# Merged activations of a hybrid decoder layer: VectorE block transposes and a trip through DRAM in place of TensorE transposes

## The chip, the cores and the metric

One core of one Trainium2 chip runs the whole kernel. The metric is the device time of one execution in microseconds. The engines are TensorE (PE in the profile; PEld is its weight load), VectorE (DVE), ScalarE (ACT), GpSimd (POOL) and SyncE (SP, which here only issues DMAs). Every engine works through its own list in order; they meet through semaphores.

## The reference, cut to what matters

One layer of three parallel token mixers over 256 tokens and 2048 channels, each projected to 2048 channels, weighted by a sigmoid gate and added; then one output projection, a residual and a norm:

```
merged = (g_sb * (o_sb @ w_branch_sb[layer])
          + g_ssd * (o_ssd @ w_branch_ssd[layer])
          + g_mem * (o_mem @ w_branch_mem[layer]))
x = x + merged @ w_out[layer]
return rms_norm(x, final_norm_w)
```

All matrices are float32. The kernel forms a product as three TensorE products of parts: `hi` is the value rounded to the type fp32r, `lo` the rest, and the sum is hi*hi + hi*lo + lo*hi.

## The kernel before, in words

**A weight product (`gemm`).** It makes 256 tokens x 512 output columns. Weights stream in chunks of two 128-row tiles (`load_chunk`, 512 KB, line 207, issued by SP into the four buffers `raw`). `split` makes `wh` on ScalarE (line 146) and `wl` on VectorE (line 150), three buffers each; then 12 matrix products follow (lines 266 to 268: with `wh`, `wl`, `wh`). A product over 2048 channels has eight chunks, called c0 to c7 below. The left operand must lie with channels on the partitions ("columns", class `Cols`, as hi and lo).

**What sets the order.** The program is written out once, and each engine keeps that order. `defer(fn, n)` puts a piece of work behind the products of the n-th next chunk; `pump()`, at the end of every chunk, runs what is due. The result of a product is fetched `LATE` = 3 chunks after its last chunk.

**The tail around the change.** The third branch goes through four groups g of 512 columns. For each group there is a gate product (from `hT`, 8 chunks) and a branch product (from `oD`, 8 chunks). `branch_evac` then multiplies the branch product by its gate on VectorE (line 857, two instructions for the two halves t of the tokens, tile `sig`) and adds it to `merged[t]` on GpSimd (line 858). `merged` has tokens on the partitions, so the output projection needs it turned. `merged_cols` does that on TensorE: eight 128x128 transposes a group (line 838, tile `mt` in PSUM), and two chunks later `split` writes `mT` (hi on ScalarE, lo on VectorE). The output projection (`w_out`) has four products over `mT`; its first product follows the branch product of group 3 at once and reads the columns of group 3 in its chunks c6 and c7, those of groups 0 to 2 in c0 to c5. The evacuation and the transposes of group g thus lie inside the first chunks of the product after it: the gate product of group g+1, or for group 3 the first product with `w_out`.

Other DMAs that ScalarE issues in this stretch are the gate bias (`sig`, line 843), the final norm's weights (`fw`, line 879) and the residual (`xr`, line 921). The results are stored at the very end (line 917).

Of the kernel before, what the change touches and what calls it, by code (L numbers as in the profile page):

```python
# [10 lines left out]
F32 = mybir.dt.float32  # L11
# [5 lines left out]
P = 128  # L17
D = 2048
T = 256
NKT = D // P  # L20
GW = 512
# [4 lines left out]
LATE = 3  # L26
# [15 lines left out]
def trunk_kernel(  # L42
# [6 lines left out]
    nc = tc.nc  # L49
# [6 lines left out]
    dram = ctx.enter_context(tc.tile_pool(name="dram", bufs=1, space=bass.MemoryType.DRAM))  # L56
# [5 lines left out]
    def nm(s):  # L62
        cnt[0] += 1
        return f"{s}_{cnt[0]}"

    def slot(shape, dt=F32, n="slot"):
        return big.tile(shape, dt, tag="slot", name=nm(n))

    def t4(shape, n="t4"):
        return tmp.tile(shape, F32, tag="t4", name=nm(n), bufs=2)  # L70
# [16 lines left out]
    def bank(shape, n="bank"):  # L87
        return psB.tile(shape, F32, tag="bank", name=nm(n))
# [11 lines left out]
    ident = const.tile([P, P], F32, name="ident")  # L100
# [41 lines left out]
    def split(*parts):  # L142


        for hi, _, src, scale in parts:
            nc.scalar.activation(hi, src, AF.Copy, **({} if scale is None else {"scale": scale}))  # L146
        for hi, lo, src, scale in parts:
            h32 = hi.bitcast(F32)
            if scale is None:
                nc.vector.tensor_tensor(lo, src, h32, ALU.subtract)  # L150
            else:
                nc.vector.scalar_tensor_tensor(lo, src, scale, h32, ALU.mult, ALU.subtract)
# [19 lines left out]
    def defer(fn, chunks=LATE):  # L172

        cnt[0] += 1
        heapq.heappush(late, (now[0] + chunks, cnt[0], fn))
# [9 lines left out]
    def pump():  # L185


        now[0] += 1
        while late and late[0][0] <= now[0]:
            heapq.heappop(late)[2]()  # L190
        advance(lanes[now[0] % 2])

    def finish():
        while lanes[0] or lanes[1]:
            for lane in lanes:
                advance(lane)
# [8 lines left out]
    def load_chunk(w, c0, width, k0, kc):  # L205
        raw = stage.tile([P, kc, width], F32, tag="raw", name=nm("raw"), bufs=RAWB)
        nc.sync.dma_start(
            raw, w[k0 * P:(k0 + kc) * P, c0:c0 + width].rearrange("(k p) n -> p k n", p=P))
        return raw
# [36 lines left out]
            nc.scalar.activation(dst, acc[:, :, 1], AF.Copy)  # L246
            nc.vector.tensor_tensor(dst, acc[:, :, 0], dst, ALU.add)

    def gemm(lhs, nk, w, c0, evac):

        acc2 = psA.tile([P, 2, GW], F32, tag="acc", name=nm("acc"), bufs=2)
        acc = [acc2[:, 0], acc2[:, 1]]
        kc = KC
        for k0 in range(0, nk, kc):
            raw = load_chunk(w, c0, GW, k0, kc)
            wh = stage.tile([P, kc, GW], F32R, tag="wh", name=nm("wh"))
            wl = stage.tile([P, kc, GW], F32R, tag="wl", name=nm("wl"))
            split((wh, wl, raw, None))
            for j in range(kc):
                kt = k0 + j  # L260
                lh, ll = lhs.at(kt)
                first, last = kt == 0, kt == nk - 1
                for t in range(2):
                    a = acc[t]
                    tt = slice(t * P, (t + 1) * P)
                    nc.tensor.matmul(a, lh[:, tt], wh[:, j], start=first, stop=False)  # L266
                    nc.tensor.matmul(a, lh[:, tt], wl[:, j], start=False, stop=False)  # L267
                    nc.tensor.matmul(a, ll[:, tt], wh[:, j], start=False, stop=last)  # L268
            pump()
        defer(lambda: evac(acc))  # L270

    def to_cols(dst, b0):

# [165 lines left out]
    for g in range(4):  # L439
        gemm_cols(memT, NKT, w_mem_kv, 2 * g * P, to_split_cols(kT, 2 * g),  # L440
                  acc=None if g else [bank([P, 2, T], "acc") for _ in range(2)])
# [161 lines left out]
    for g in range(2):  # L603
        gemm(hT, NKT, w_in, C_SBV + g * GW, to_rows(vS, g * GW))
# [226 lines left out]
    merged = [slot([P, D], F32, "merged") for _ in range(2)]  # L831
    mT = []

    def merged_cols(k0):
        ps = bank([P, 2, T], "mt")
        for j in range(2):
            for t in range(2):
                nc.tensor.transpose(ps[:, j, t * P:(t + 1) * P],  # L838
                                    merged[t][:, (k0 + j) * P:(k0 + j + 1) * P], ident)
        defer(lambda: split((*mT[0].at(k0, 2), ps, None)), 2)  # L840

    def gate_evac(c0, sig):
        nc.scalar.dma_start(sig[:, 0], b_gate[c0:c0 + GW].partition_broadcast(P))
        def evac(acc):
            for t in (1, 0):
                nc.vector.tensor_tensor(sig[:, t], acc[t], sig[:, 0], ALU.add)
            defer(lambda: sigmoid(sig), 1)
        return evac

    def branch_evac(br, g, sig):  # L850
        cs = slice(g * GW, (g + 1) * GW)
        def evac(acc):
            for t in range(2):
                if br == 0:
                    nc.vector.tensor_tensor(merged[t][:, cs], acc[t], sig[:, t], ALU.mult)
                else:
                    nc.vector.tensor_tensor(sig[:, t], acc[t], sig[:, t], ALU.mult)  # L857
                    nc.gpsimd.tensor_tensor(merged[t][:, cs], merged[t][:, cs], sig[:, t],  # L858
                                            ALU.add)
            if br == 2:  # L860
                for pr in range(2):
                    defer(lambda pr=pr: merged_cols(4 * g + 2 * pr), 1)
        return evac

    branches = ((4096, oM, 8, w_branch_mem), (0, oS, 8, w_branch_sb), (2048, None, 16, w_branch_ssd))
    for br, (g0, src, nk, wb) in enumerate(branches):
        for g in range(4):
            sig = t4([P, 2, GW], "sig")
            gemm(hT, NKT, w_in, C_GATE + g0 + g * GW, gate_evac(g0 + g * GW, sig))
            if src is None:  # L870
                finish()
                mT.append(Cols(NKT, "mT"))
                src = oD[0]
            gemm(src, nk, wb, g * GW, branch_evac(br, g, sig))


    yo = [slot([P, D], F32, "yo") for _ in range(2)]
# [58 lines left out]
    g = 3  # L936
# [9 lines left out]
    for t in range(2):  # L946
        tt = slice(t * P, (t + 1) * P)
        for cs in (slice(0, GW),) if t == 0 else (slice(0, T), slice(T, GW)):
            acc = psA.tile([P, 2, GW], F32, tag="acc", name=nm("acc"),
                           bufs=2)[:, 0, 0:cs.stop - cs.start]  # L950
# [50 lines left out]
```

## Time and profile before

| | |
|---|---|
| time of the runs | 1227.94 us median of 3 (1227.71 to 1228.21) |
| span of the profiled execution | 1226.6 us, so 1.3 us below the median time |
| TensorE busy, of the span | 99% |
| VectorE, ScalarE, GpSimd busy | 64%, 53%, 4% |
| mean granted TensorE clock | 0.998 |
| from memory | 239.48 MB, 197 GB/s over the span |

The profile gives for the execution itself only its span; what a run takes beyond it (1.3 us) is the start and the end that the trace does not hold. In the page's groups, `out<-in` names the tile that is written and those that are read; "idle before" is what the engine waited just ahead of an instruction, and the arrow says for whom. The times of matrix products overlap (0.39 us each, one begun every 0.23 us), so the distance between starts is their price, not their duration.

### The profile page before, as it was taken

How to read it: one execution, taken by the hardware profiler on the slowest of the kernel's cores; microseconds unless marked ns; L12 is line 12 of the kernel's file. 1: busy time of each engine (PE TensorE's matmuls, PEld its weight loads, DVE VectorE, ACT ScalarE, POOL GpSimd, SP SyncE). 2: the span in 40 equal slices, each digit the busy share in tenths (PEclk: the TensorE clock that was granted, in tenths of full speed). 3: DMA queues.
4: the chain of work that ended last, by engine and by line, in shares of the span. 5: the costliest groups of instructions: out<-in, count | busy, mean ns of one | idle time of the engine just before them, and what ended most of it. 6: DMA issues, size and time to landing. Idle time of an engine off the chain costs nothing.

```text
span 1226.6 us, 16569 instructions
## 1 busy us (share of the span) xinstructions
PE 1215.5 (99%) x6388; PEld 1034.8 (84%) x6388; DVE 784.2 (64%) x990; ACT 649.1 (53%) x875; POOL 51.2 (4%) x50
## 2 busy tenths in 40 slices
PE   9999999999999999999999999999999999999997
PEld 7888888888888888888888888888888888888886
DVE  5686554565654555888888758676777755555554
ACT  6765443554445454545665756475756544444443
POOL 0000000000000000010100000000000010110101
PEclk9999999999999999999999999999999999999999
DMA  9966566655566656565567667686766666567673
GB/s 340 342 197 187 163 194 189 187 168 165 166 180 182 187 172 182 169 182 173 177 185 223 207 200 218 180 231 181 231 184 192 202 195 205 188 197 240 204 240 107
DMA packets 175023, 242.70 MB, mean 198 GB/s; under 512 B 10272, under 2 KB 109792, under 8 KB 174816
## 3 DMA queue, kind: packets, MB, share of 16 engines
q1 hardware_dynamic: 168224, 229.51, 61.2%
q10 hardware_dynamic: 6720, 12.13, 3.0%
q8 instruction: 50, 0.82, 0.3%
q14 instruction: 29, 0.24, 0.1%
HBM read 239.48 MB, written 2.13 MB: 197 GB/s over the span
## 4 chain that ended last, share of the span: by engine, by line
PE 96%; DMA 1%; issue 1%; DVE 1%; ACT 1%; SPq 0%; POOLq 0%; POOL 0%; ACTq 0%
PE acc L229 29%; PE acc L266 15%; PE acc L267 15%; PE acc L268 15%; PE acc L233 14%; PE acc L398 1%; PE acc L399 1%; PE acc L397 1%; PE y L773 1%; DMA raw<-in_w_out_dram 1%; DMA raw<-in_w_mem_kv_dram 1%; PE dtp L459 0%; PE xp L730 0%; PE mt L838 0%; PE spo L649 0%
## 5 line engine op out<-in xcount | busy, mean ns | idle before, releaser
L150 DVE TENSOR_TENSOR wl<-raw,wh 128x1024 fp32r<-128x1024 f32 (+1 forms) x409 | 502.8, 1233 | 310.3 <-ACT wh L146 308.1
L146 ACT ACTIVATE wh<-raw 128x1024 fp32r<-128x1024 f32 (+1 forms) x409 | 431.0, 1055 | 382.5 <-PE acc L268 200.7
L229 PE MATMUL acc<-hT,wh 128*128 128x512 f32 x1408 | 444.0, 397 | 0.0
L233 PEld LDWEIGHTS acc<-hT,wl 128*128 128x128 f32 x1408 | 264.5, 188 | 62.5
L233 PE MATMUL acc<-hT,wl 128*128 128x256 f32 x1408 | 276.8, 278 | 0.0
L229 PEld LDWEIGHTS acc<-hT,wh 128*128 128x128 f32 x1408 | 214.4, 189 | 0.1
L266 PE MATMUL acc<-wh,hT 128*128 128x512 f32 x448 | 175.9, 393 | 0.0
L267 PE MATMUL acc<-wl,hT 128*128 128x512 f32 x448 | 174.7, 390 | 0.0
L268 PE MATMUL acc<-wh,hT 128*128 128x512 f32 x448 | 174.6, 390 | 0.0
L266 PEld LDWEIGHTS acc<-wh,hT 128*128 128x128 f32 x448 | 84.1, 188 | 17.7 <-ACT sq L146 0.5
L268 PEld LDWEIGHTS acc<-wh,hT 128*128 128x128 f32 x448 | 84.1, 188 | 17.8
L267 PEld LDWEIGHTS acc<-wl,hT 128*128 128x128 f32 x448 | 84.1, 188 | 17.4 <-DVE wl L150 0.6
L266 PE MATMUL acc<-wh,oD 128*128 128x512 f32 x128 | 49.8, 389 | 0.0
L267 PE MATMUL acc<-wl,oD 128*128 128x512 f32 x128 | 49.8, 389 | 0.0
L268 PE MATMUL acc<-wh,oD 128*128 128x512 f32 x128 | 49.8, 389 | 0.0
L687 DVE SCALAR_TENSOR_TENSOR cT<-cu,wcols,cT 128x255 f32<-128x255 f32 (+2 forms) x96 | 46.4, 483 | 3.4
L858 POOL TENSOR_TENSOR merged<-merged,sig 128x512 f32<-128x512 f32 x16 | 25.1, 1588 | 521.9 <-DVE sig L857 521.9
L229 PE MATMUL acc<-memT,wh 128*128 128x512 f32 x128 | 40.5, 398 | 0.0
L266 PE MATMUL acc<-wh,mT 128*128 128x512 f32 x96 | 37.4, 390 | 0.0
L268 PE MATMUL acc<-wh,mT 128*128 128x512 f32 x96 | 37.4, 389 | 0.0
L267 PE MATMUL acc<-wl,mT 128*128 128x512 f32 x96 | 37.4, 389 | 0.0
L630 POOL TENSOR_TENSOR lm<-lm,sp 128x384 f32<-128x384 f32 x8 | 13.1, 1639 | 394.7 <-DVE sp L629 385.0
(250 smaller groups left out, 1301.4 us busy)
## 6 DMA issues: line engine op xcount, KB each, us to landing
raw<-in_w_in_dram SPq DMA_DIRECT2D x288, 512.0 KB, 3.8
raw<-in_w_branch_ssd_dram SPq DMA_DIRECT2D x32, 512.0 KB, 4.1
raw<-in_w_out_dram SPq DMA_DIRECT2D x32, 512.0 KB, 5.1
raw<-in_w_mem_kv_dram SPq DMA_DIRECT2D x31, 512.0 KB, 6.6
raw<-in_w_branch_mem_dram SPq DMA_DIRECT2D x16, 512.0 KB, 4.1
raw<-in_w_branch_sb_dram SPq DMA_DIRECT2D x16, 512.0 KB, 4.5
dec<-acT SPq DMA_DIRECT2D x24, 256.0 KB, 6.2
sig<-in_b_gate_dram ACTq DMA_DIRECT2D x12, 256.0 KB, 4.7
```

The lines of the kernel that those rows point to most:

```text
L146: nc.scalar.activation(hi, src, AF.Copy, **({} if scale is None else {"scale": scale}))
L150: nc.vector.tensor_tensor(lo, src, h32, ALU.subtract)
L229: nc.tensor.matmul(halves[b], wh[:, kt - k0, b * P:(b + 1) * P], lhs.both(kt), start=first, stop=False, skip_group_check=True)
L233: nc.tensor.matmul(halves[b][:, 1], wl[:, kt - k0, b * P:(b + 1) * P], lhs.at(kt)[0], start=False, stop=last, skip_group_check=True)
L266: nc.tensor.matmul(a, lh[:, tt], wh[:, j], start=first, stop=False)
L267: nc.tensor.matmul(a, lh[:, tt], wl[:, j], start=False, stop=False)
L268: nc.tensor.matmul(a, ll[:, tt], wh[:, j], start=False, stop=last)
L397: nc.tensor.matmul(a, lh[:, tt], wh[:, g], start=first, stop=False)
L398: nc.tensor.matmul(a, lh[:, tt], wl[:, g], start=False, stop=False)
L630: nc.gpsimd.tensor_tensor(lm, lm, sp, ALU.subtract)
L687: nc.vector.scalar_tensor_tensor(a[:, s:T], u[:, 0:T - s], convw[:, 3 - s, i:i + 1], a[:, s:T], ALU.mult, ALU.add)
L858: nc.gpsimd.tensor_tensor(merged[t][:, cs], merged[t][:, cs], sig[:, t], ALU.add)
```

## The change

The eight transposes on TensorE go. In their place, for every group: two block transposes on VectorE (`turn`), which turn each 32x32 block in place of its 128x128 tile and write them in the order (t, j, k, c); one DMA of 512 KB to a scratch tensor in DRAM (`away`); four DMAs of 128 KB back, one for each band of 32 partitions (`back`), which put the blocks where a full transpose would have them; and the same split into `mT`, as four pieces of 256 columns in place of two of 512. Runs of 128 numbers (512 bytes) are contiguous in the read back. ScalarE issues all five DMAs. For group 3 alone the evacuation is done two chunks after the product, not three.

```
-    def gemm(lhs, nk, w, c0, evac):
+    def gemm(lhs, nk, w, c0, evac, chunks=LATE):
...
-        defer(lambda: evac(acc))
+        defer(lambda: evac(acc), chunks)
...
-    def merged_cols(k0):
-        ps = bank([P, 2, T], "mt")
-        for j in range(2):
-            for t in range(2):
-                nc.tensor.transpose(ps[:, j, t * P:(t + 1) * P],
-                                    merged[t][:, (k0 + j) * P:(k0 + j + 1) * P], ident)
-        defer(lambda: split((*mT[0].at(k0, 2), ps, None)), 2)
+    turned = [dram.tile([2, P, 4, 4, 32], F32, name=f"turned{i}") for i in range(4)]
+
+    def turn(g):
+
+        pair = slot([P, 2, 1024], F32, "turn")
+        blocks = pair[:, 0].rearrange("p (t j k c) -> p t j k c", t=2, j=4, k=4)
+        cols = pair[:, 1].rearrange("p (i k c) -> p i k c", i=8, k=4)
+        for t in range(2):
+            nc.vector.transpose(blocks[:, t].rearrange("p j k c -> p k j c"),
+                                merged[t][:, g * GW:(g + 1) * GW]
+                                .rearrange("p (k j c) -> p k j c", k=4, j=4))
+
+        def away():
+            nc.scalar.dma_start(turned[g].rearrange("t p j k c -> p t (j k c)"),
+                                blocks.rearrange("p t j k c -> p t (j k c)"))
+
+        def back():
+            for j in range(4):
+                nc.scalar.dma_start(
+                    cols[32 * j:32 * j + 32].rearrange("r i k c -> r i (k c)"),
+                    turned[g][:, :, j].rearrange("t (i r) k c -> r (t i) (k c)", r=32))
+            for k in range(4):
+                defer(lambda k=k: split((*[a.rearrange("p (i c) -> p i c", c=32)
+                                           for a in mT[0].at(4 * g + k)],
+                                         cols[:, :, k], None)), 1 + k // 2)
+        defer(away, 1)
+        defer(back, 2)
...
-                for pr in range(2):
-                    defer(lambda pr=pr: merged_cols(4 * g + 2 * pr), 1)
+                defer(lambda: turn(g), 1)
...
-            gemm(src, nk, wb, g * GW, branch_evac(br, g, sig))
+            gemm(src, nk, wb, g * GW, branch_evac(br, g, sig), 2 if br == 2 and g == 3 else LATE)
```

Where it puts things on ScalarE, in the gate product after group 0's branch product (the splits of the chunks c3 to c7 are the rows `wh`, and the last `wh` is c0 of the product after it). Before:

```order
L146 ACTIVATE wh_8741<-raw_8739 128x1024
L146 ACTIVATE wh_8769<-raw_8767 128x1024
L146 ACTIVATE wh_8787<-raw_8785 128x1024
L146 ACTIVATE mT_8526<-mt_8757 128x2x256
L146 ACTIVATE mT_8526<-mt_8762 128x2x256
L146 ACTIVATE wh_8809<-raw_8807 128x1024
L146 ACTIVATE wh_8827<-raw_8825 128x1024
```

And now:

```order
L146 ACTIVATE wh_8745<-raw_8743 128x1024
L146 ACTIVATE wh_8766<-raw_8764 128x1024
L847 DMA turned_5981<-turn_8761 128x2x512
L146 ACTIVATE wh_8785<-raw_8783 128x1024
L852 DMA turn_8761<-turned_5981 32x8x128 x4
L146 ACTIVATE wh_8807<-raw_8805 128x1024
L146 ACTIVATE mT_8530<-turn_8761 128x256 x2
L146 ACTIVATE wh_8829<-raw_8827 128x1024
L146 ACTIVATE mT_8530<-turn_8761 128x256 x2
L146 ACTIVATE wh_8852<-raw_8850 128x1024
```

Here wh_8745 is c3, so `away` stands behind the split of c4, the four reads behind that of c5, and the first pieces of `mT` behind that of c6 and ahead of that of c7.

On VectorE, in the first product with `w_out`, after group 3 (`sig` is the multiplication by the gate, `wl` the splits of the chunks from c1 on). Before:

```order
L150 TENSOR_TENSOR wl_9647<-raw_9644,wh_9646 128x1024
L150 TENSOR_TENSOR wl_9665<-raw_9662,wh_9664 128x1024
L857 TENSOR_TENSOR sig_9304<-acc_9469,sig_9304 128x512 x2
L150 TENSOR_TENSOR wl_9687<-raw_9684,wh_9686 128x1024
L150 TENSOR_TENSOR wl_9715<-raw_9712,wh_9714 128x1024
L150 TENSOR_TENSOR wl_9733<-raw_9730,wh_9732 128x1024
L150 TENSOR_TENSOR mT_8529<-mt_9702,mT_8529 128x2x256
L150 TENSOR_TENSOR mT_8529<-mt_9707,mT_8529 128x2x256
L150 TENSOR_TENSOR wl_9755<-raw_9752,wh_9754 128x1024
```

And now:

```order
L150 TENSOR_TENSOR wl_9657<-raw_9654,wh_9656 128x1024
L877 TENSOR_TENSOR sig_9312<-acc_9479,sig_9312 128x512 x2
L150 TENSOR_TENSOR wl_9679<-raw_9676,wh_9678 128x1024
L842 STREAM_TRANSPOSE turn_9694<-merged_5979 128x4x4x32
L842 STREAM_TRANSPOSE turn_9694<-merged_5980 128x4x4x32
L150 TENSOR_TENSOR wl_9700<-raw_9697,wh_9699 128x1024
L150 TENSOR_TENSOR wl_9719<-raw_9716,wh_9718 128x1024
L150 TENSOR_TENSOR wl_9741<-raw_9738,wh_9740 128x1024
L150 TENSOR_TENSOR mT_8533<-turn_9694,mT_8533 128x256 x2
L150 TENSOR_TENSOR wl_9763<-raw_9760,wh_9762 128x1024
L150 TENSOR_TENSOR mT_8533<-turn_9694,mT_8533 128x256 x2
```

The multiplication stands one chunk earlier, the block transposes stand behind the split of c2 and ahead of that of c3, and the pieces of `mT` behind the splits of c5 and c6. The lists of GpSimd and SP are the same as before.

## The prediction

> **What bounds the kernel now.** I read the busy times and the chain of waits first, then the tile `mt`, then the order of time on each engine where the transposes stand, and last the DMA issues.
>
> ```profile
> PE 1215.5 (99%) x6388; PEld 1034.8 (84%) x6388; DVE 784.2 (64%) x990; ACT 649.1 (53%) x875; POOL 51.2 (4%) x50
> ...
> PE 96%; DMA 1%; issue 1%; DVE 1%; ACT 1%; SPq 0%; POOLq 0%; POOL 0%; ACTq 0%
> ```
>
> TensorE is busy all along, and the chain that ends last is TensorE for 96% of the span. A piece of work taken off TensorE's list therefore shortens the time by what it takes there, as long as nothing makes TensorE wait instead. The transposes are such a piece:
>
> ```profile
> L838 PE MATMUL mt<-ident,merged x32: 270/272/273, 1005.8 to 1139.8; 128*128 128x128 f32 x32
> ...
> 1005.60 0.40 PE L268 MATMUL acc<-wh,hT 128*128 128x512 f32 x1
> 1005.84 1.04 PE L838 MATMUL mt<-ident,merged 128*128 128x128 f32 x8
> 1006.63 0.48 PE L266 MATMUL acc<-wh,hT 128*128 128x512 f32 x1
> 1006.95 0.40 PE L267 MATMUL acc<-wl,hT 128*128 128x512 f32 x1
> ...
> 1138.85 0.39 PE L268 MATMUL acc<-wh,mT 128*128 128x512 f32 x1
> 1139.08 1.03 PE L838 MATMUL mt<-ident,merged 128*128 128x128 f32 x8
> 1139.87 0.48 PE L266 MATMUL acc<-wh,mT 128*128 128x512 f32 x1
> 1140.19 0.40 PE L267 MATMUL acc<-wl,mT 128*128 128x512 f32 x1
> ```
>
> Products start 0.23 us apart (1006.63 follows by a larger step only because of the eight transposes). Without them the L267 at 1006.95 would start two steps of 0.227 after 1005.60, at 1006.06; so a group costs 0.89 us, and the fourth one too (1140.19 against 1139.30). **What is removed: 4 x 0.89 = 3.56 us**, or 0.29% of the time. It cannot be more: this is the floor of the new time, 1227.94 - 3.56 = 1224.4. The kernel's runs spread over 0.5 us; I take 0.2%, 2.46 us, as what a measurement tells from no change.
>
> **The new chain and how much time it has.** Everything that is added lies beside TensorE. What matters is when ScalarE and VectorE can split the next weight chunk. Group 0, in time from the span's start:
>
> ```profile
> 997.39 1.28 DVE L857 TENSOR_TENSOR sig<-acc,sig 128x512 f32<-128x512 f32 x2
> 998.96 1.65 DVE L150 TENSOR_TENSOR wl<-raw,wh 128x1024 fp32r<-128x1024 f32 x1 [0.30 <-ACT wh L146]
> 1001.68 1.23 DVE L150 TENSOR_TENSOR wl<-raw,wh 128x1024 fp32r<-128x1024 f32 x1 [1.07 <-ACT wh L146]
> ...
> 998.24 3.53 POOL L858 TENSOR_TENSOR merged<-merged,sig 128x512 f32<-128x512 f32 x2 [40.82 <-DVE sig L857]
> ...
> 1000.59 1.06 ACT L146 ACTIVATE wh<-raw 128x1024 fp32r<-128x1024 f32 x1 [1.66 <-PE acc L268]
> 1003.31 1.06 ACT L146 ACTIVATE wh<-raw 128x1024 fp32r<-128x1024 f32 x1 [1.66 <-PE acc L268]
> ```
>
> The splits of c3 and c4 on VectorE start at 998.96 and 1001.68, those of c4 and c5 on ScalarE at 1000.59 and 1003.31: one chunk is 2.72 us, of which ScalarE works 1.06 and waits 1.66 for TensorE to free a buffer. GpSimd ends its two additions at 1001.77. c3's last product is the L268 at 1005.60; without transposes c4 starts at 1005.83 and c7 three chunks later, at 1013.99, and its second product, which reads `wl`, at 1014.22.
>
> Now the new order. The block transposes stand behind the split of c3, which ends at 1000.61. No row shows a block transpose; one half is 128x512 float32 on VectorE, so I bound it by two rows of that size and take 0.69, near the SBUF sum, since it reads and writes memory just as that does:
>
> ```profile
> L914 DVE TENSOR_SCALAR yo<-yo,frs 128x512 f32<-128x512 f32 x4 | 1.8, 480 | 0.0
> L745 DVE TENSOR_TENSOR dec<-dec,cmask 128x512 f32<-128x512 f32 x16 | 11.6, 763 | 0.0
> L150 DVE TENSOR_TENSOR oS<-so,oS 128x256 fp32r<-128x256 f32 x8 | 3.4, 425 | 3.9 <-ACT oS L146 3.9
> L146 ACT ACTIVATE oS<-so 128x256 fp32r<-128x256 f32 x8 | 3.3, 418 | 14.7 <-DVE so L655 14.7
> ```
>
> The first half runs beside GpSimd's second addition and stretches it by some 0.3 us (c3's split beside it took 1.65 instead of 1.23, so the two hinder each other). The second starts at about 1002.1 and ends at 1002.8. Between 0.48 and 0.76 a half this moves by 0.3 us at most. c4's split on VectorE slips by 1.1 us to 1002.8, ends at 1004.0, and is needed at 1006.06: hidden. `away` is issued at 1002.8 and lands a us later. The four reads wait for that on ScalarE, with the split of c6 behind them (it would start at 1006.03 by TensorE's pace, and may start as late as 1008.9); their last lands b us after the first is issued. Then come, in ScalarE's order, two pieces of `mT` (0.42 each), c7's `wh` (1.06) and on VectorE c7's `wl` (1.23): with the hand-over 3.16 us, so TensorE waits at c7 if the data land later than 1014.22 - 3.16 = 1011.06. With 0.1 us of hand-over between the DMAs **the round trip a + b has 8.2 us.** The remaining two pieces and c0 of the next product end 2.2 us later, inside c7's 2.72 us: no second wait.
>
> Group 3 has the same order with everything one chunk earlier:
>
> ```profile
> 1127.97 0.39 PE L268 MATMUL acc<-wh,oD 128*128 128x512 f32 x1
> ...
> 1130.91 1.28 DVE L857 TENSOR_TENSOR sig<-acc,sig 128x512 f32<-128x512 f32 x2
> ...
> 1131.77 3.53 POOL L858 TENSOR_TENSOR merged<-merged,sig 128x512 f32<-128x512 f32 x2 [41.16 <-DVE sig L857]
> ```
>
> TensorE is done with the product at 1128.4, and VectorE now multiplies at once, not behind c2's split at 1130.91. GpSimd starts 0.86 after VectorE and takes 3.53: 1132.8, with the stretch 1133.1; the second half ends at 1133.8. c6 would start at 1139.08 + 2 x 2.72 = 1144.52, its `wl` is needed at 1144.75, less 3.16 is 1141.59: **7.7 us**. The earlier evacuation itself costs nothing: c2's split (1.23 us) that it pushes back is not needed before 1133.9.
>
> **How long the round trip takes.** No row shows a store of 512 KB or a read of 512-byte pieces from ScalarE's queue. The nearest rows:
>
> ```profile
> raw<-in_w_branch_ssd_dram SPq DMA_DIRECT2D x32, 512.0 KB, 4.1
> ...
> sig<-in_b_gate_dram ACTq DMA_DIRECT2D x12, 256.0 KB, 4.7
> ...
> xr<-in_x_dram ACTq DMA_DIRECT2D x4, 512.0 KB, 6.8
> ...
> out_dram<-yo SPq DMA_DIRECT2D x4, 256.0 KB, 3.2
> out_dram<-yo ACTq DMA_DIRECT2D x4, 192.0 KB, 2.8
> ...
> out_dram<-yo SPq DMA_DIRECT2D x2, 128.0 KB, 2.1
> ...
> L921 ACTq DMA_DIRECT2D xr<-in_x_dram x4: 374/406/447, 1120.6 to 1186.4; - x4
> ```
>
> The number at the end is the microseconds to landing; the last row has the nanoseconds that ScalarE's queue takes to issue `xr`. The first row is a weight load on SP's queue; `sig` and `xr` are reads on ScalarE's queue beside such loads; the stores come at the end of the kernel. Single ones: `raw` between 1000 and 1012 us, `xr` at 1143.0, the three `sig` of this stretch:
>
> ```profile
> DMA to landing us min/median/max: 3.5/3.7/4.0
> ...
> DMA to landing us min/median/max: 5.6/5.6/5.6
> ...
> DMA to landing us min/median/max: 4.8/5.0/5.3
> ```
>
> a lies between 2.8 (192 KB stored) and 5.6 (512 KB on that queue beside two weight loads). I take 3.6, by `raw` of the same bytes and rows of 2 KB: the load ahead of it was issued when c3's split ended (1000.6) and is nearly through, the next follows at 1004. b is three more issues at 0.4 and the landing of the last: 1.2 + 2.1 at the least (a 128 KB store), 1.2 + 5.3 at the most (`sig`). I take 1.2 + 3.5 = 4.7, by the quickest `raw`, which moves as many bytes as the four together. The pieces are 512 bytes where the weights have 2 KB or, in the column products, 1 KB:
>
> ```profile
> 100.00:130.00 30.00, 30.00 (x185) 26.64 (x184) 16.82 (x19) 13.08 (x16) 0.00 (x0) 1.00 0.62 177
> ...
> 1010.00:1030.00 20.00, 20.00 (x90) 16.57 (x89) 10.08 (x10) 9.10 (x9) 0.00 (x0) 1.00 0.59 189
> ```
>
> The last two columns are the DMA share and GB/s: 285 GB/s at full share with 1 KB, 320 with 2 KB, or 57 and 102 ns a piece on one of 16 engines; on that line 512 bytes take 35 ns, and 64 pieces an engine 2.2 us against 1.6 for a weight chunk. That fits into 3.5.
>
> **The sum.** x = a + b = 8.3 us. Groups 0 to 2 wait 3 x (8.3 - 8.2) = 0.3, group 3 0.6: 0.9 in all; above 8.2 the wait is 4x - 32.3. 3.56 - 0.9 = 2.66, so the span goes from 1226.6 to 1223.9 and the time, 1.3 us above it, from 1227.94 to **1225.3 us**.
>
> Costed at nothing: on VectorE per group 2 x 0.69 + 4 x 0.42 in place of 2 x 0.69 (it idles over a microsecond a chunk), on ScalarE 4 x 0.42 in place of 2 x 0.60 and five issues (cover: its 1.66 us of waiting a chunk). SP's list is the same. A weight load is issued when VectorE ends the split four chunks before: the one of the next product's c0 at 1004.0, for ScalarE's split at 1011.5 at the earliest; even at `xr`'s 5.6 us it is there in time. GpSimd's additions gate nobody but the transposes. The start and the tail of the kernel do not change.
>
> **Rivals.** *The trip takes back more, but not all* (x from 8.35 to 9.58): the same wait at c7, 1.1 to 6.0 us in all, and a time within 0.2% of before, 1225.5 to 1230.4. For it: both reads on ScalarE's queue, `sig` and `xr`, are slower than `raw`. Against it: the stores on it are quick.
>
> *Slower: ScalarE, held by the last read, lets TensorE run out of weights.* Place: c7 of three gate products and c6 of the first `w_out` product. Point from which it decides: x = 8.97 eats the gain; from 9.58 it shows. With a at `xr`'s 5.6 and b at 4.7, x is 10.3: the wait 8.9, the time 1233.3. For it: one DMA hangs on the other and both on one in-order engine, and the budget leaves nothing over. Against it: both at their slow ends is needed, or one wholly.
>
> *The small pieces are dear.* If a piece of 512 bytes takes an engine as long as one of 2 KB, 64 x 102 ns = 6.5 us instead of 2.2: b = 9.0, x = 12.6, the wait 18.1, the time 1242.5. Against it: the step from 2 KB to 1 KB cost 11% of rate, not half. [...]
>
> **Chances.** Forecast (x to 8.35, its own range 1224.4 to 1225.5) 0.42; part taken back 0.33; slower by ScalarE 0.18; dear pieces 0.05, strides 0.02. Faster 0.42, same 0.33, slower 0.25. Below 1224.0 lies nearly nothing (the floor and half a spread); above 1233.5, x over 10.3, I leave 0.06 of the slower case and both last ones. Range 1224.0 to 1233.5.
>
> **What would show it.** TensorE with 32 instructions less and no gap where they stood. `turn` in VectorE's list at about 0.7 us a half. `turned` landing in 3.6 us and the last `turn` 4.7 after the first is issued. A wait of TensorE for `wl` at c7 of about 0.1 us, at c6 after group 3 of 0.6. ScalarE's `mT` waiting for the DMA, not for TensorE. The prediction is wrong if a block transpose takes over 1.5 us, if the read back lands its four parts one after the other, or if the weight loads get late.

## The result, and the profile after

The changed kernel takes 1243.62 us (median of four runs, 1243.23 to 1243.98) against 1227.83 for the kernel before (four runs, 1227.71 to 1228.21): the ratio is 1.0125, 95% interval 1.0114 to 1.0137, so it is slower, and clear of the noise. Forecast was 1225.3 with a range of 1224.0 to 1233.5. The span grew from 1226.6 to 1242.0 us.

From the page of the changed kernel, the busy times and the chain that ended last:

```profile
PE 1219.3 (98%) x6356; PEld 1033.8 (83%) x6356; DVE 788.6 (63%) x1006; ACT 649.1 (52%) x883; POOL 52.2 (4%) x50
...
PE 85%; DMA 7%; ACT 2%; DVE 2%; issue 2%; POOL 1%; ACTq 1%; SPq 0%; POOLq 0%
```

TensorE has the 32 instructions less that the edit promised, and yet is busy 3.8 us longer: many of its products last longer (the 448 of line 267 over `hT` 394 ns in the mean, before 390). The chain is no longer TensorE alone; 7% of it are DMAs. The instructions that touch the tile `turn`:

```profile
L852 ACTq DMA_DIRECT2D turn<-turned x16: 319/472/869, 1007.2 to 1153.5; - x16
...
L842 DVE STREAM_TRANSPOSE turn<-merged x8: 697/706/712, 1001.8 to 1145.5; 128x512 f32<-128x512 f32 x8
```

A block transpose of 128x512 takes 0.71 us. That is not the trouble. ScalarE and TensorE in order of time, after group 0 (start, duration, and in brackets the idle time ahead and who ended it):

```profile
1003.78 0.38 ACTq L847 DMA_DIRECT2D turned<-turn  x1
1004.59 1.06 ACT L146 ACTIVATE wh<-raw 128x1024 fp32r<-128x1024 f32 x1 [1.70 <-PE acc L268]
1007.21 1.84 ACTq L852 DMA_DIRECT2D turn<-turned  x4
1009.15 1.06 ACT L146 ACTIVATE wh<-raw 128x1024 fp32r<-128x1024 f32 x1 [3.50 <-issue]
1015.22 0.72 ACT L146 ACTIVATE mT<-turn 128x256 fp32r<-128x256 f32 x2 [5.00 <-DMA turn<-turned]
1015.85 1.04 ACT L146 ACTIVATE wh<-raw 128x1024 fp32r<-128x1024 f32 x1
...
1016.94 0.49 PE L266 MATMUL acc<-wh,hT 128*128 128x512 f32 x1 [1.55 <-ACT wh L146]
1018.20 0.50 PE L267 MATMUL acc<-wl,hT 128*128 128x512 f32 x1 [0.76 <-DVE wl L150]
```

`away` is issued at 1003.78 and the reads at 1007.21, so the store took a = 3.4 us. The splits of `mT` start at 1015.22: from the first issue of the reads to the last landing b = 8.0 us. ScalarE stands still for 5.0 us with the next weights' split behind it in its list, and TensorE waits for these, first for `wh` and then for `wl`. Groups 1 and 2 are alike, with b = 8.7 and 8.6 us. In group 3 of this profile it is the store that is late, a = 5.8, and b is 5.2. The landing times between 1003 and 1012 us:

```profile
raw<-in_w_branch_ssd_dram SPq DMA_DIRECT2D x3, 512.0 KB, 4.9
turned<-turn ACTq DMA_DIRECT2D x1, 512.0 KB, 3.4
turn<-turned ACTq DMA_DIRECT2D x4, 128.0 KB, 6.4
```

TensorE's and ScalarE's waits over the whole tail (us in total, times, longest):

```profile
PE acc L266 <- ACT wh L146: 6.5, 4, 2.2
PE acc L267 <- DVE wl L150: 3.7, 5, 0.8
...
ACT mT L146 <- DMA turn<-turned: 17.8, 4, 5.5
```

These gaps make 10.2 us, and by the distances below the waits cost 12 us, in the main because a gap is counted from the end of a product, which lasts longer (0.39 us) than the step from one product to the next (0.23). The rest is the clock. Stretches of 2 us after group 2; the third number from the right is the granted clock of TensorE:

```profile
1112.00:1114.00 2.00, 0.85 (x2) 0.51 (x3) 1.60 (x3) 2.00 (x5) 0.00 (x0) 0.69 0.00 0
1114.00:1116.00 2.00, 2.00 (x6) 1.54 (x6) 2.00 (x3) 0.88 (x1) 0.00 (x0) 0.50 0.56 165
1116.00:1118.00 2.00, 2.00 (x6) 1.63 (x5) 0.56 (x1) 0.00 (x0) 0.00 (x0) 0.50 0.79 224
1118.00:1120.00 2.00, 2.00 (x7) 1.54 (x7) 0.14 (x1) 1.06 (x1) 0.00 (x0) 0.60 0.85 284
```

Behind the gap TensorE runs at half clock for some 6.8 us: 0.31 + 0.50 + 0.50 + 0.40, times 2 us, is 3.4 us lost. After group 1 it is 1.7 us by the same reckoning, after groups 0 and 3 nothing.

A useful measure for what follows is the distance from the first gate product after a group to the first branch product behind it. Without transposes and waits it is 21.76 us (sixteen 128-row tiles of weights at 1.36). Before and after, for group 0:

```profile
994.95 0.39 PE L266 MATMUL acc<-wh,hT 128*128 128x512 f32 x1
...
1017.61 0.39 PE L266 MATMUL acc<-wh,oD 128*128 128x512 f32 x1
```

```profile
996.18 0.39 PE L266 MATMUL acc<-wh,hT 128*128 128x512 f32 x1
...
1020.86 0.39 PE L266 MATMUL acc<-wh,oD 128*128 128x512 f32 x1
```

Before it is 22.66, that is 0.90 for the transposes; after it is 24.68, a loss of 2.9. In the same way groups 1 to 3 lose 5.0, 6.2 (with what the slow clock took from the product behind it) and 3.0: 17.1 in all, of which 5.1 are clock. Less the 3.56 gained, 13.5. The other 1.9 of the span's 15.4 us lie outside the change: this profile reaches the first gate product 1.2 us later, and its last output group ends 0.7 later. Kernels that are equal up to that gate product reach it anywhere from 994.6 to 996.9 us, so the 1.2 is scatter.

### The profile page after: what moved, and what is told of

Its sections match the earlier page's. It is cut to its first block, busy times and chain, and to the rows that moved or that the text cites. A ratio compares the mean times of both kernels' runs of the same rounds, so it can differ in the third digit from the quotient of the medians.

```text
span 1242.0 us, 16561 instructions
## 1 busy us (share of the span) xinstructions
PE 1219.3 (98%) x6356; PEld 1033.8 (83%) x6356; DVE 788.6 (63%) x1006; ACT 649.1 (52%) x883; POOL 52.2 (4%) x50
## 4 chain that ended last, share of the span: by engine, by line
PE 85%; DMA 7%; ACT 2%; DVE 2%; issue 2%; POOL 1%; ACTq 1%; SPq 0%; POOLq 0%
PE acc L229 29%; PE acc L233 14%; PE acc L267 13%; PE acc L266 13%; PE acc L268 13%; DMA rows<-in_mem_dram 1%; DMA turned<-turn 1%; ACT wh L146 1%; DMA rows<-in_x_dram 1%; DMA raw<-in_w_branch_ssd_dram 1%; PE y L773 1%; DVE wl L150 1%; POOL merged L878 1%; DMA raw<-in_w_out_dram 1%; DMA raw<-in_w_mem_kv_dram 1%
```

## The experiments

At first I blamed the pieces of 512 bytes (theory A), with three rivals: the bands of 32 partitions (B), data that have only just been written (C), the sharing with the weight loads (D); and a fifth (E), that the added work itself slows the groups. Four kernels came first.

**The early evacuation alone**, in the kernel before:

```
-            gemm(src, nk, wb, g * GW, branch_evac(br, g, sig))
+            gemm(src, nk, wb, g * GW, branch_evac(br, g, sig), 2 if br == 2 and g == 3 else LATE)
```

> This kernel is the kernel before with one part of the change alone: the last branch group is evacuated a piece sooner, the transposes stay on TensorE. Theory (the trip through DRAM costs everything, the earlier evacuation is free): no difference, 1225.5 to 1230.3 us around 1227.8, and the first gate product after group 0 starts where it does in the kernel before (994.95 us by its profile). Rival (the earlier evacuation itself makes a wait, because merged is read from the accumulators a piece sooner by VectorE and GpSimd): 1229 to 1232 us.

Measured: 1228.54 against 1228.21 us, ratio 0.9999 (0.999 to 1.0008). This part of the change is free.

**Larger pieces**, in the changed kernel:

```
-                    cols[32 * j:32 * j + 32].rearrange("r i k c -> r i (k c)"),
-                    turned[g][:, :, j].rearrange("t (i r) k c -> r (t i) (k c)", r=32))
+                    pair[32 * j:32 * j + 32, 1].rearrange("r (t f) -> r t f", t=2),
+                    turned[g][:, 32 * j:32 * j + 32].rearrange("t r j k c -> r t (j k c)"))
```

> The changed kernel with the same four reads back in the same four bands of 32 partitions and the same bytes, but in pieces of 2 KB instead of 512 bytes; the columns then hold the block-turned rows as they were stored and not the transposed ones. Theory A (the small pieces keep the DMA engines busy for twice the time their bytes need, beside two weight loads): first issue to last landing falls from 8.0 to 8.7 us to about 5 us in groups 0 to 2, the sum of both trips from 11.4 to 12.1 us to about 8.5, TensorE's waits at the chunk of ScalarE's wh shrink from 1.55 to 2.21 us to under 0.5, and the time is 1226 to 1232 us. Theory B (four reads on bands of 32 partitions, each held to a part of the engines, whatever the piece): first issue to last landing stays at about 8 us and the time at 1242 to 1245 us.

Measured: 1244.37 us (1240.69 to 1246.85), ratio 1.0128 (1.0107 to 1.0148), and between 1003 and 1012 us

```profile
turn<-turned ACTq DMA_DIRECT2D x4, 128.0 KB, 6.4
```

Of this window the landing is the same as with 512 bytes. Over the groups b is 7.9, 7.0, 7.3 and 8.8 us: in groups 0 to 2 it is 0.1, 1.7 and 1.3 us shorter than in the changed kernel's first profile, not the 3 us and more that theory A expected, and the median time is no better. Theory A has fallen as the main cause: my own first reading of the trace, that the engines are busy because the pieces are short, was wrong.

**Nobody waits in groups 0 to 2**:

```
-                                         cols[:, :, k], None)), 1 + k // 2)
-        defer(back, 2)
+                                         cols[:, :, k], None)),
+                      1 + k // 2 if g == 3 else 4 + k)
+        defer(back, 2 if g == 3 else 4)
```

> The changed kernel with the read back of groups 0 to 2 issued at 4 chunks after the turn and their splits at 4 to 7 chunks after that, so that nobody needs the data soon; the last group as in the changed kernel. All the transposes, DMAs and splits stay. Theory A (what costs is that the in-order ScalarE waits for the read back before it makes the next weights): no TensorE wait in groups 0 to 2, no drop of the granted clock there, and only the 3.65 us of the last group is lost: 1227.83 - 3.56 + 3.65 = 1227.9 us, or 1229.1 if the 1.24 us that the changed kernel was late already before group 0 are seen again. Rival E (the added work itself, DMA traffic in small pieces or instructions on VectorE and ScalarE, slows the groups whenever it runs): 1235 to 1240 us.

Measured: 1232.62 us, ratio 1.0036 (1.0026 to 1.0047), above both expectations of A and below E. In groups 0 to 2 the distance is 21.76 us to the hundredth, with each of the same reads still landing in 6.5 us (median): the added work costs nothing there, and all 3 x 0.90 us of the transposes are gained. E has fallen. The one wait for `wh` that is left is that of group 3, and it is longer than in the first profile (b 9.4 instead of 5.2), with a clock drop behind it, so group 3 alone loses 7.5 us, where it lost 3.0 in the first profile:

```profile
PE acc L266 <- ACT wh L146: 3.4, 1, 3.4
```

**Groups 0 to 2 through DRAM without a wait, the last group on TensorE**: the edit above, and

```
-                defer(lambda: turn(g), 1)
+                if g < 3:
+                    defer(lambda: turn(g), 1)
+                else:
+                    for pr in range(2):
+                        defer(lambda pr=pr: merged_cols(4 * g + 2 * pr), 1)
```

with `LATE` for every group again.

> Groups 0 to 2 by block transposes and the trip through DRAM, read back at 4 chunks as in the run with nobody waiting; the last group by TensorE transposes and evacuated as in the kernel before. Theory A: the gain of three groups' transposes alone remains, 1227.83 - 3 x 0.89 = 1225.2 us (1226.4 if the late start of 1.24 us is seen again), no wait of TensorE beyond the kernel before's. Rival E (the added work costs wherever it runs): 1233 to 1237 us.

Measured: 1225.41 us against 1228.21, ratio 0.9978 (0.9968 to 0.9987). It beats the kernel before by 2.8 us, which is what three groups of transposes cost (3 x 0.90).

**What a trip costs by itself.** Behind the end of the kernel before, single round trips, each `trip(name, form, loads beside)`:

```
+    old = trip("a_warm", one_2k, False)
+    trip("b_bands_short", bands_512, False)
+    trip("c_bands_long", bands_2k, False)
+    trip("d_one_short", one_512, False)
+    trip("e_one_long", one_2k, False)
+    trip("f_bands_short", bands_512, True)
...
+    trip("i_one_long", one_2k, True)
+    trip("", bands_512, False, old)
+    trip("", bands_512, True, old)
```

> The kernel before with eleven round trips through DRAM added behind its end, one after the other, where nothing else runs: 512 KB stored from one tile, then read back in one of four forms (four bands of 32 partitions or one transfer over 128 partitions, each in pieces of 512 bytes or of 2 KB), first with the queues empty, then with two weight loads of 512 KB released by the same landing; at last the band form from data stored long before, without and with the two loads. Its time is that of the kernel before plus the trips, some 70 to 120 us; only the single trips are read. Theory D (what makes the read back late is the sharing with the weight loads, whatever its form): alone every form takes 2.5 to 4.5 us from first issue to the last landing, with two loads beside it 5.5 to 8 us, bands and single transfers alike. Theory B (bands of 32 partitions): the bands take over 1.5 times what the single transfer of the same pieces takes, with and without loads. Theory A (small pieces): the 512-byte forms take over 1.5 times what the 2 KB forms take; the run with bands of 2 KB pieces speaks against it already. Theory C (data just stored is slow to read): the trips from old data take over 1 us less than those from new data.

Measured, for the bands of 512 bytes alone and with two loads: the issue of the reads, and the instruction on VectorE that waits for all of them (for f its wait is for the bands, not for the loads):

```profile
1234.02 1.84 ACTq L968 DMA_DIRECT2D trip<-b_bands_short  x4
...
1238.44 1.22 DVE L996 TENSOR_TENSOR trip<-trip 128x1024 f32<-128x1024 f32 x1 [7.61 <-DMA trip<-b_bands_short]
...
1266.59 1.83 ACTq L968 DMA_DIRECT2D trip<-f_bands_short  x4
...
1275.58 1.23 DVE L996 TENSOR_TENSOR trip<-trip,more 128x1024 f32<-128x1024 f32 x1 [11.85 <-DMA trip<-f_bands_short]
```

4.4 us alone, 9.0 with two loads. The four forms, each a single trip of one execution, in us from the first issue:

| read back of 512 KB | alone | with two loads |
|---|---|---|
| one transfer, 2 KB pieces | 3.6 | 5.9 |
| one transfer, 512-byte pieces | 4.2 | 6.7 |
| bands, 2 KB pieces | 4.1 | 8.8 |
| bands, 512-byte pieces | 4.4 | 9.0 |
| bands, 512-byte pieces, old data | 4.6 | 9.2 |

(Of the single transfers with loads the time to landing stands there, since the loads came last.) C has fallen: old data are no quicker. D is true for every form, and B only in company: bands cost under half a us on empty queues and over 2 beside loads. Part of these 2 us is the order of issue: the single transfer goes out before both loads, two of the four bands after them. Until the read and both loads were all there it took 8.8 to 9.0 us with bands and 7.4 with a single transfer.

**A single transfer over 128 partitions** in the changed kernel, in pieces of 2 KB (the edit shown) and of 512 bytes:

```
-            for j in range(4):
...
+            nc.scalar.dma_start(
+                pair[:, 1].rearrange("p (t f) -> p t f", t=2),
+                turned[g].rearrange("t p j k c -> p t (j k c)"))
```

> The changed kernel with the read back as a single transfer of 512 KB over all 128 partitions in pieces of 2 KB, the most favourable form; the columns then hold the rows as they were stored and not the transposed ones. Theory B (bands of 32 partitions): first issue to landing falls from 8 us to 4 to 5 us, TensorE's waits for the weights to under 0.5 us a group, and the time is 1226 to 1231 us. Theory D (sharing with the weight loads): three issues of 0.45 us each are saved, first issue to landing is still 6 to 7 us, ScalarE still waits, and the time is 1232 to 1241 us.

> The changed kernel with the read back as a single transfer over all 128 partitions, in pieces of 512 bytes as in the changed kernel; the columns then hold blocks in another arrangement and not the transposed rows. Theory B: as with 2 KB pieces, 4 to 5 us and 1226 to 1231 us. Theory D: 6 to 7 us and 1232 to 1241 us. If the pieces count after all, this one is slower by over 2 us than the same transfer in 2 KB pieces.

Measured: 1230.62 us, ratio 1.002 (1.0011 to 1.003), with 2 KB, and 1233.68, ratio 1.0043 (1.0028 to 1.0058), with 512 bytes. From the first issue to the splits it is 5.6 to 6.1 us in groups 0 to 2 with 2 KB, and 6.8 to 7.2 with 512 bytes. The first time is what B expected and the second what D did, and the landings are later than B's 4 to 5 us: both are at work. The 512-byte pieces cost a single transfer 0.7 to 1.5 us of b in these groups and 3.1 us of the time, more than the 2 us that were to show that they count: they are a smaller cause beside the other two. In the windows where the DMA engines are all busy, the first row is of the changed kernel (bands), the second of the single transfer with 2 KB; the last two numbers are the DMA share and GB/s (the share can pass 1, since a packet is counted whole where it starts):

```profile
1011.00:1012.00 1.00, 1.00 (x6) 0.84 (x5) 0.47 (x1) 0.00 (x0) 0.00 (x0) 1.00 1.21 225
```

```profile
1010.00:1011.00 1.00, 1.00 (x6) 0.84 (x5) 0.00 (x0) 0.00 (x0) 0.00 (x0) 1.00 1.04 381
```

With bands the engines are as busy and move 186 GB/s per full share in this microsecond, not 366. It is one of the bands' low rows: between 1009 and 1014 us they have 182 to 308, the single transfer between 1009 and 1012 us 363 to 374.

**The span of partitions alone.** Those two kernels also have one issue where the change has four. So, at last, four reads as before, but each over all partitions:

```
-                    cols[32 * j:32 * j + 32].rearrange("r i k c -> r i (k c)"),
-                    turned[g][:, :, j].rearrange("t (i r) k c -> r (t i) (k c)", r=32))
+                    cols[:, 2 * j:2 * j + 2].rearrange("p t k c -> p t (k c)"),
+                    turned[g][:, :, j].rearrange("t p k c -> p t (k c)"))
```

> The changed kernel with four reads back of 128 KB in 512-byte pieces as before, but each over all 128 partitions and a quarter of the columns, not over 32 partitions and all of them; the columns then hold the blocks in another arrangement and not the transposed rows. Issues, bytes and pieces are those of the changed kernel, the span of partitions alone differs. Theory B (32 partitions: the engines need longer for a byte): first issue to last landing 7.0 to 7.6 us instead of 8.0 to 8.7, over 330 GB/s at full DMA share where the bands have 190 to 300, and 1230 to 1236 us. Rival (four issues in place of one made the difference between this form and the single transfers): 8.0 to 8.7 us and 1240 to 1246 us.

Measured: 1233.89 us, ratio 1.0044 (1.0029 to 1.0058), and after group 0

```profile
1006.41 1.95 ACTq L852 DMA_DIRECT2D turn<-turned  x4
...
1013.04 0.73 ACT L146 ACTIVATE mT<-turn 128x256 fp32r<-128x256 f32 x2 [3.52 <-DMA turn<-turned]
```

b is 6.6, 6.9, 6.7 and 6.8 us, 1.4 to 1.9 less than with bands in groups 0 to 2, for the same bytes, pieces and issues, and the time is 9.7 us below the changed kernel's. It is also that of the single transfer in 512-byte pieces, so the rival, four issues in place of one, has fallen. Per full DMA share, all transfers together move 290 to 360 GB/s between 1008 and 1011 us, not everywhere over 330 as expected; in the changed kernel it is 180 to 310 between 1009 and 1014. So beside the loads the bands cost these 1.4 to 1.9 us; on empty queues, with four bands in flight, the landing is only 0.2 to 0.5 us later than that of a single transfer over all partitions. Why a band is slower, no run shows.

**No large loads beside the read**, bands and small pieces kept:

```
-            raw = load_chunk(w, c0, GW, k0, kc)
+            raw = load_chunk(w, c0, P if thin else GW, k0, 1 if thin else kc)
```

> The changed kernel with the weight loads thinned that run beside the read back: the SSD branch's products of groups 1 to 3 and the first output group load 64 KB a chunk instead of 512 KB and split it eight times over, so ScalarE, VectorE and TensorE have the same instructions and only the bytes are gone (the products are then with other weights). Theory D with B (sharing with the loads sets the landing, the bands cost little without them): first issue to last landing 4.3 to 5 us instead of 8.0 to 8.7, both trips together 7.5 to 8.6 us, no wait of TensorE over 0.4 us a group and no drop of the clock: 1227.9 - 3.56 = 1224.4, up to 1226.5 us. Rival (the read back is slow in this place whatever runs beside it): 8 us as before and 1241 to 1245 us.

Measured: 1227.97 us, ratio 1.0002 (0.9993 to 1.0011), and after group 0

```profile
1003.48 0.38 ACTq L851 DMA_DIRECT2D turned<-turn  x1
...
1006.95 1.84 ACTq L856 DMA_DIRECT2D turn<-turned  x4
...
1011.41 0.72 ACT L146 ACTIVATE mT<-turn 128x256 fp32r<-128x256 f32 x2 [1.46 <-DMA turn<-turned]
```

b is 4.5, 4.5 and 4.7 us in groups 0 to 2, and all three keep the 21.76 us. The total missed 1224.4 because of group 3: the thin loads were through so early that SP had full ones of the next output group on the way again (five of 512 KB between 1134 and 1150 us, two of them on the way while the reads were), b was 7.8, and TensorE waited and lost clock once more:

```profile
1134.72 3.47 ACTq L856 DMA_DIRECT2D turn<-turned  x4
...
1142.48 0.73 ACT L146 ACTIVATE mT<-turn 128x256 fp32r<-128x256 f32 x2 [3.14 <-DMA turn<-turned]
```

So the same code in one run shows both: 4.5 us without large loads beside it, 7.8 with them, where the four issues alone took 1.6 us longer.

**The clock.** Eight products of 128x128 that nobody reads, ahead of the late chunk:

```
+    def fill(n):
+        fw_ = bank([P, P], "fill")
+        for _ in range(n):
+            nc.tensor.matmul(fw_, ones, ones, start=True, stop=True)
...
+        defer(lambda: fill(FILL), 3 if g < 3 else 2)
```

> The changed kernel with eight products of 128x128 into a bank that nobody reads put on TensorE ahead of the chunk whose weights come late (the last of the gate product; in the last group the chunk before). They fill about 2 to 2.7 us of the wait. Clock theory (the gap itself lowers the granted clock for the next 4 to 8 us and so costs as much again): no window under 0.95 after groups 1 and 2, and the time falls by 3 to 7 us against the changed kernel, to 1236.5 to 1240.5. Rival (the clock is no consequence of the gap, or its loss is hidden by the weights that are late anyway): 1242 to 1246 us, or more where the products outlast the wait.

Measured: 1240.63 us, ratio 1.0094 (1.0077 to 1.0111). No clock drop after groups 0 to 2, where the waits left were under 0.8 us each; in group 3 the spare products stood a chunk too early, a wait of 2.28 us remained and the clock fell for 6.8 us. So they were moved to where that wait came, and the changed kernel was run beside them:

```
-        defer(lambda: fill(FILL), 3 if g < 3 else 2)
+        defer(lambda: fill(FILL if g < 3 else FILL + 4), 3)
```

> As the kernel with eight spare products ahead of the late chunk, but in the last group they stand at the chunk where the wait came in that run, and are twelve. Clock theory: no wait over 2 us is left, so no window of half clock in any group, and the time falls by the 3.4 us that the drop after the last group cost in that run: 1236 to 1239 us. Rival (the clock follows something else): as before, 1240 to 1244 us.

> The changed kernel once more, on the same chip as the two others. All theories: 1242 to 1246 us. Clock theory: in each group with a wait of TensorE of over 2 us by the trace the clock falls to 0.5 for about 3.4 or 6.8 us, and in groups with a wait under 1.9 us it does not.

Measured: 1239.15 us (1236.56 to 1240.64) with the spare products, 1245.44 (1242.68 to 1246.4; ratio 1.0139, 1.0124 to 1.0154) without: more work on TensorE, and 6.3 us less time. By the windows the profile of the one loses 1.7 us to the clock, of the other 8.5. But my rule of 2 us of waiting failed on both sides. In the changed kernel's second profile, group 0 kept its clock and group 3 did not:

```profile
1017.11 0.50 PE L266 MATMUL acc<-wh,hT 128*128 128x512 f32 x1 [2.38 <-ACT wh L146]
1018.37 0.51 PE L267 MATMUL acc<-wl,hT 128*128 128x512 f32 x1 [0.76 <-DVE wl L150]
...
1160.52 0.80 PE L266 MATMUL acc<-wh,mT 128*128 128x512 f32 x1 [2.88 <-ACT wh L146]
```

and with the spare products one wait of 1.5 us was followed by a drop, as were one of 1.1 us (reads over all partitions, group 3) and one of 0.8 (thin loads, group 3). Over all these profiles 8 of 9 waits for `wh` of over 2 us were followed by a drop, and of 25 groups with shorter waits 3. Every one of these drops took some 3.4 or 6.8 us. In the first profile the half clock lasts from 1064.98 to 1068.39 us after group 1 and from 1112.76 to 1119.59 after group 2, so 3.413 us and twice that. In each of these traces the granted clock changes only at whole multiples of this length after its first rise (in the first profile at 310, 311, 324, 326 and 360 of them, in the second at 310, 312, 325, 326, 338, 340 and 361). Cut into such stretches, the changed kernel's second profile shows why the two waits fared differently. Here are two stretches each after groups 0 and 3; the first number behind the length is TensorE's busy time, the third from the right the clock:

```profile
1013.23:1016.64 3.41, 1.50 (x7) 0.92 (x5) 0.76 (x2) 1.25 (x3) 0.00 (x0) 1.00 0.34 95
1016.64:1020.06 3.42, 2.19 (x8) 1.61 (x9) 2.97 (x5) 2.93 (x5) 0.00 (x0) 1.00 0.14 46
...
1156.59:1160.00 3.41, 1.05 (x5) 0.55 (x3) 0.75 (x2) 1.20 (x3) 0.00 (x0) 1.00 0.26 74
1160.00:1163.41 3.41, 2.42 (x5) 1.63 (x6) 2.92 (x5) 2.97 (x5) 0.00 (x0) 0.50 0.59 182
```

After group 0 the idle time is split into 1.9 and 1.2 us, and the clock stays; after group 3 one stretch has 2.4 us, and the next runs at half clock. Over all these profiles, the 8 stretches at full clock with 2.1 us idle or more were all followed by half clock, 3 of the 7 with 1.53 to 1.91 us, and none with less. So the idle time summed within one stretch sorts the drops better than the length of a wait: the three behind short waits are the three in the middle. What decides between 1.5 and 2.1 us stays open, and no run moved a gap of one length from stretch to stretch.

## Why the prediction was wrong, point by point

*The gain, 3.56 us, 0.89 a group.* Right: 0.90 in each group without a wait, and 2.8 us by the timed ratio with three groups.

*The block transposes, 0.69 a half, the early evacuation at nothing, the other added work hidden.* Right: 0.71; 0.9999; and 21.76 us a group when nobody waits.

*The store, a = 3.6.* Right: 3.4, though 5.8 once, after group 3.

*The read back, b = 4.7.* **This is the step that failed.** It measured 8.0 to 8.7 in groups 0 to 2, above the upper bound of 6.5, and in group 3 5.2 in the first profile and 9.0 in the second. The bands without large loads took 4.4 to 4.7: I had priced the trip for a free queue. I took the landing of the quickest weight load, 3.5 us, while two or three weight loads of 512 KB are on the way in the same 8 us. Beside loads, four reads over all partitions take 6.6 to 6.9, some 2.2 more than the bands without large loads, and with bands of 32 partitions the DMA engines stay as busy and move less, which adds 1.4 to 1.9 more. My upper bound, `sig`, did share the queue, but writes all partitions, so it held no band. The rival that small pieces are dear had a time near the result, 1242.5, by luck: it put 4.3 us of b on the pieces, and longer pieces shortened b by 0.1 to 1.7 us in groups 0 to 2, in bands and in a single transfer. The chances also leave a fiftieth to strides; no run shows a price for them, and b was never above 9.4 us in the groups given here.

*The budget, 8.2 us, and a wait of x less 8.2 a group.* Right in kind, 0.3 to 1.0 us too dear each time. Reads over all partitions had x of 10.1 to 10.4 and lost 1.5 to 1.8; the single transfer with 2 KB had 9.3 to 9.8 and lost 0.7 to 1.3; x of 7.9 lost nothing. With the measured x of 11.4, 12.1, 12.0 and 11.0 the formula gives 14.2 us of waiting, where 11.9 were lost without the clock. So what came is the rival in which ScalarE, held by the last read, lets TensorE run out of weights, at the place that it named and with x beyond its 10.3. It had put a at fault; in groups 0 to 2 it was b, and only in group 3 of the first profile was it mostly a (5.8, with b = 5.2).

*A wait of TensorE costs its own length.* Wrong, and in no rival: the sum put the clock at nothing, and it added 5.1 us in the first profile and 8.5 in the second.

The sum with the measured terms is -3.56 + 11.9 + 5.1, or 13.5 us for the change, and 15.4 with the 1.9 outside the four groups, as the spans differ; the medians differ by 15.8.

## What to carry to other kernels

Price a new transfer beside the loads that will be in flight at that moment, by a row that spans the same partitions, and not by the quickest row of its size: the bands here took 4.4 to 4.7 us without large loads beside them and 8.0 to 8.7 with them. A wait for a DMA on an engine that also feeds TensorE is paid by everything behind it in that list (after group 0 it was 5.0 us of ScalarE, and the group lost 2.9): issue the transfer early, put the work that needs it several chunks later, and where the data are needed at once, as after the last group here, keep the method without a trip (1225.4 us with it, 1232.6 with the trip). TensorE's waits of over 2 us cost 1.7 or 3.4 us more for the clock in 8 of 9 cases here: compare that with a few spare products in the gap, which took 6.3 us off the time.

## What the runs showed of the hardware that I had not expected

- Bands of 32 partitions cost nearly nothing on empty queues (4.1 against 3.6 us for 512 KB) and a good deal beside other loads (8.8 against 5.9, in part by the order of issue), and the second of the two loads then lands after 7.3 to 7.4 us instead of 6.8. In the kernel, at the same number of issues, they cost 1.4 to 1.9 us a read.
- Waits of TensorE of 2.1 to 3.4 us, with a second of 0.5 to 0.8 behind the first product, were followed in 8 of 9 cases by 3.4 or 6.8 us at half clock, a loss of 1.7 or 3.4 us. The clock changed only in steps of 3.413 us, and 2.1 us or more of idle time within one such stretch were followed by a drop in 8 of 8 cases. Spare products in the gap made the kernel 6.3 us quicker.
- Data written to DRAM just before are read no slower than old ones (4.4 against 4.6 us, in one trip each).
